# The first three stores of a streaming gradient kernel move from the SP queue to the ACT queue

## The chip, the cores and the metric

The kernel runs on one core of a Trainium2 chip. The metric is the device time of one execution in microseconds (us), as the median of several runs. Times of single steps come from one profiled execution, whose clock starts at the first instruction.

## The reference

The input `x` is a matrix of 8192 x 8192 float32 numbers, drawn at random. The result has the same shape and type.

```python
def reference(x: np.ndarray) -> np.ndarray:
    return np.gradient(x, axis=1)
```

`np.gradient` along a row means: in the inside of the row, half the difference of the right and the left neighbour; in the first column `x[1] - x[0]`, in the last column `x[m-1] - x[m-2]`. Every number of `x` is read once and every result is written once, 268.44 MB each way.

## The kernel before, in words

**Tiles.** The 8192 rows are cut into 32 tiles of 256 rows. A tile lies on 128 partitions with two whole rows on each (R = 2, m = 8192), so that one partition holds 16384 numbers, or 64 KB. One tile is 8.39 MB. A load brings a whole tile in one DMA (line 60), and a store takes a whole tile out in one DMA (line 89).

**Slots.** There are three buffers, slot0, slot1 and slot2 (NB = 3). Tile i lives in slot i mod 3. The result is written in place: a slot has 64 columns of margin in front (SH = 64), the input lies behind the margin, and the result starts at column 0. So a slot must be stored completely before the next tile can be loaded into it. `load(k)` therefore waits for the store of tile k - 3.

**The steps of one tile.** First, GpSimd (POOL) subtracts the two pairs of numbers at the row ends, for both rows, into the small tile `ends` (line 70). It waits for the load. Then VectorE (DVE) runs one custom instruction over the whole tile, half the difference of the neighbours, 128 x 16382 numbers (line 76). It also writes wrong numbers where one row meets the next, and at the row ends. Then either DVE or POOL copies `ends` over the row ends (line 87; `placer` says which of the two). Then the store is issued, which waits for that copy.

**The order of the work.** Inside `tc.manual_schedule()` each engine runs its instructions in the order in which the program text gives them. `chain` records by hand which earlier step each instruction must wait for. All 64 DMAs are issued by SyncE (SP). On SP the order is: loads 0, 1, 2, then stores 0, 1, 2, then loads 3, 4, 5, then stores 3, 4, 5, and so on, three loads and three stores in turn, up to loads 30, 31 and stores 30, 31. SP takes its instructions in order: an instruction that waits holds all that stand behind it. The loads of the next group stand behind the third store of a group because the source issues them there:

```python
if i % NB == NB - 1:
    for k in range(i + 1, min(i + 1 + NB, nsets)):
        load(k)
```

The ACT engine has no instruction of its own in this kernel, and TensorE has none either.

Of the kernel before, what the change touches and what calls it, by code (L numbers as in the profile page):

```python
# [1 line left out]

# [4 lines left out]


@with_exitstack
def kernel(  # L10
    ctx: ExitStack,
    tc: tile.TileContext,
    x: bass.AP,
    out: bass.AP,
):

    nc = tc.nc
    P = nc.NUM_PARTITIONS
    n, m = x.shape
    R = 2
    NB = 3  # L30
    SH = 64
    W = R * m
    nsets = n // (P * R)
    f32 = x.dtype

    x_sets = x.rearrange("(s p t) m -> s p (t m)", p=P, t=R)
    out_sets = out.rearrange("(s p t) m -> s p (t m)", p=P, t=R)

    pool = ctx.enter_context(tc.tile_pool(name="pool", bufs=1))
    slots = [pool.tile([P, SH + W], f32, name=f"slot{k}", tag=f"slot{k}") for k in range(NB)]  # L40
    ends = pool.tile([P, nsets, R, 2], f32, name="ends", tag="ends")
    loads, stores = [], [None] * nsets
    in_front = {}

    def chain(i, ins, *needed):

        group, engine = f"slot{i % NB}", ins.ins.engine
        keep = [o.ins for o in needed]  # L50
        if in_front.get(engine, (None,))[0] == group:
            keep.append(in_front[engine][1])
        tc.declare_no_dep(ins.ins, group=group, keep=keep, reason="implied by the needed step")
        tc.add_to_no_dep_group(group, ins.ins)
        in_front[engine] = group, ins.ins
        return ins

    def load(i):
        b = slots[i % NB]
        ins = nc.sync.dma_start(out=b[:, SH : SH + W], in_=x_sets[i])  # L60
        loads.append(chain(i, ins, *([stores[i - NB]] if i >= NB else [])))

    with tc.manual_schedule():
        for i in range(NB):
            load(i)
        for i in range(nsets):
            b = slots[i % NB]
            xin = b[:, SH : SH + W].rearrange("p (t m) -> p t m", m=m)

            ins = nc.gpsimd.tensor_sub(  # L70
                out=ends[:, i, :, :],
                in0=xin[:, :, 1 : m : m - 2],
                in1=xin[:, :, 0 : m - 1 : m - 2],
            )
            at = [chain(i, ins, loads[i])]
            ins = nc.vector._custom_dve(  # L76
                dve_ops.TENSOR_TENSOR_REDUCE_SUB_MAX,
                out=b[:, 1 : W - 1],
                in0=b[:, SH + 2 : SH + W],
                in1=b[:, SH : SH + W - 2],  # L80
                s0=0.0,
                s1=0.5,
            )
            halved = chain(i, ins, *at)
            res = b[:, 0:W].rearrange("p (t m) -> p t m", m=m)
            placer = nc.gpsimd if i % 5 in (1, 3) and i < nsets - 2 else nc.vector
            ins = placer.tensor_copy(out=res[:, :, 0 : m : m - 1], in_=ends[:, i, :, :])  # L87
            placed = chain(i, ins, halved)
            ins = nc.sync.dma_start(out=out_sets[i], in_=b[:, 0:W])
            stores[i] = chain(i, ins, placed)  # L90
            if i % NB == NB - 1:
                for k in range(i + 1, min(i + 1 + NB, nsets)):
                    load(k)


# [1 line left out]
_INS = ['x']  # L97
_OUTS = [((8192, 8192), 'float32')]


# [23 lines left out]
```

## Time and profile before

| what | value |
|---|---|
| median of 3 runs | 1247.86 us (1247.66 to 1247.92) |
| span of the profiled execution, first to last instruction | 1245.7 us |
| moved by DMA | 268.44 MB read and 268.44 MB written, mean 431 GB/s |
| DVE busy | 554.6 us, 45% of the span |
| POOL busy | 8.8 us, 1% of the span |
| one custom DVE instruction (line 76), 32 of them | 17.22 us each |
| issuing one DMA on SP | 0.34 us |

The page gives the profiled execution's own time as its span alone. The median of the runs lies 2.2 us above that span, which is what lies around the first and the last instruction. A difference that is worked out in the span is therefore added to the median.

How to read it: a line of the timeline has the start in us, the duration in us, the engine, the line of the source and the operation. "SPq" is the sequencer of SP, which only issues DMAs; a row "x3" is three issues merged, from the start of the first to the end of the third. "POOL ends L70" is the first step of a tile, and its start is within 0.1 us of the landing of the tile's load, whenever POOL was waiting for it. A DMA queue's row has the number of packets, the MB, and the time that its packets took as a share of what the 16 DMA engines have in the span.

### The profile page before, as it was taken

The page shows a single profiled execution, that of the slowest core. Times are in us where ns is not written, and L with a number is a line of the kernel's source. Part 1 is how long each engine was busy: PE and PEld are TensorE (multiplying, and loading weights), DVE is VectorE, ACT ScalarE, POOL GpSimd, SP SyncE. Part 2 cuts the span into 40 slices and gives each one's busy share as a digit, 9 for nine tenths or more (in the row PEclk, how much of TensorE's full clock was granted, in tenths as well). Part 3 has the DMA queues.
Part 4 walks back from the last instruction along what each step waited for, and adds up shares of the span by engine and source line. Part 5 has one row for each costly group of instructions (what it writes and reads, how often), then busy time and mean ns, then how long its engine had stood idle before and what let it go on. Part 6 is the DMA issues. An engine that isn't in the chain of part 4 may idle for free.

```text
span 1245.7 us, 237 instructions
## 1 busy us (share of the span) xinstructions
DVE 554.6 (45%) x52; POOL 8.8 (1%) x48
## 2 busy tenths in 40 slices
DVE  2850583069009702850582079009603840591083
POOL 0000000000000000000000000000000000000000
DMA  9999999999999999999999999999999999999999
GB/s 404 438 436 423 427 431 438 438 438 436 436 427 431 425 438 436 425 434 436 429 434 436 434 436 434 436 434 438 419 436 436 434 438 438 431 434 429 429 410 404
DMA packets 9217, 536.88 MB, mean 431 GB/s; under 512 B 1024, under 2 KB 1024, under 8 KB 1024
## 3 DMA queue, kind: packets, MB, share of 16 engines
q1 hardware_dynamic: 9216, 536.88, 99.8%
q14 instruction: 1, 0.01, 0.0%
HBM read 268.44 MB, written 268.44 MB: 431 GB/s over the span
## 4 chain that ended last, share of the span: by engine, by line
another core or an unknown queue 74%; DVE 18%; DMA 3%; issue 2%; POOL 1%; SPq 0%; POOLq 0%
DVE slot L76 18%; DMA slot<-in_x_dram 3%; POOL ends L70 0%; POOL slot L87 0%; SPq L60 0%; POOLq L119 0%; DVE slot L87 0%
## 5 line engine op out<-in xcount | busy, mean ns | idle before, releaser
L76 DVE CUSTOM_DVE_ANT_0 slot<-slot 128x16382 f32<-128x16382 f32 x32 | 551.2, 17224 | 668.7 <-POOL ends L70 668.7
L70 POOL TENSOR_TENSOR ends<-slot 128x4 f32<-128x4 f32 x32 | 6.3, 198 | 989.6 <-DMA slot<-in_x_dram 989.6
L87 POOL COPY slot<-ends 128x4 f32<-128x4 f32 x12 | 2.3, 190 | 207.9 <-DVE slot L76 207.9
L87 DVE COPY slot<-ends 128x4 f32<-128x4 f32 x20 | 3.4, 172 | 0.7
L108 POOL MEMSET const-bfloat16-1.0<- 128x1 bf16 x1 | 0.1, 101 | 0.0
L108 POOL MEMSET const-uint8-127<- 128x1 uint8 x1 | 0.1, 101 | 0.0
L108 POOL MEMSET const-float32-0.0<- 128x1 f32 x1 | 0.1, 98 | 0.2 <-issue 0.2
L108 POOL MEMSET const-float32-1.0<- 128x1 f32 x1 | 0.1, 98 | 0.0
## 6 DMA issues: line engine op xcount, KB each, us to landing
slot<-in_x_dram SPq DMA_DIRECT2D x32, 58.0
out_dram<-slot SPq DMA_DIRECT2D x32, 40.4
```

Of the source, the lines that this page charges most:

```text
L70: ins = nc.gpsimd.tensor_sub(out=ends[:, i, :, :], in0=xin[:, :, 1 : m : m - 2], in1=xin[:, :, 0 : m - 1 : m - 2],)
L76: ins = nc.vector._custom_dve(dve_ops.TENSOR_TENSOR_REDUCE_SUB_MAX, out=b[:, 1 : W - 1], in0=b[:, SH + 2 : SH + W], in1=b[:, SH : SH + W - 2],
L87: ins = placer.tensor_copy(out=res[:, :, 0 : m : m - 1], in_=ends[:, i, :, :])
L108: nc = _bacc.Bacc("TRN2", target_bir_lowering=False, num_devices=1)
```

## The change

The stores of tiles 0, 1 and 2 are issued by the ACT engine instead of SP. All other stores stay on SP. The waits are the same as before: store i still waits for the row ends to be placed, and load i + 3 still waits for store i. Because the three stores are gone from SP, loads 3, 4 and 5 now stand directly behind loads 0, 1 and 2 there, each with its wait for its store. Behind load 5 come stores 3, 4, 5, and from there on the order is that of before. On ACT there are the three stores and nothing else.

```diff
             placed = chain(i, ins, halved)
-            ins = nc.sync.dma_start(out=out_sets[i], in_=b[:, 0:W])
+            queue = nc.scalar if i < NB else nc.sync
+            ins = queue.dma_start(out=out_sets[i], in_=b[:, 0:W])
             stores[i] = chain(i, ins, placed)
```

Empty lines were taken out as well, so that the line numbers of the changed kernel are smaller: its loads are on line 49, its stores on line 79, the custom DVE instruction on line 65, the first POOL step on line 59.

## The prediction

> **What bounds the kernel now.** I read the engines and the DMA queues on the page first, then the queue's waits, then the timeline of SP and POOL, then windows of the opening.
>
> ```profile
> DVE 554.6 (45%) x52; POOL 8.8 (1%) x48
> DMA packets 9217, 536.88 MB, mean 431 GB/s; under 512 B 1024, under 2 KB 1024, under 8 KB 1024
> q1 hardware_dynamic: 9216, 536.88, 99.8%
> ```
>
> One queue, q1, carries all 64 transfers, and its packets fill 99.8% of the 16 DMA engines' time. No compute engine is above 45%. Of the 9216 packets 1024 are tiny, which leaves 8192 of 536.88 MB / 8192 = 65.5 KB: a partition's 64 KB is one packet, and a transfer is 128 of them, eight on each DMA engine (with one tiny one behind).
>
> ```profile
> SPq L60 <- DMA out_dram<-slot: 373.1, 29, 19.3
> 0.74 1.33 SPq L60 DMA_DIRECT2D slot<-in_x_dram  x3
> 40.40 40.06 SPq L89 DMA_DIRECT2D out_dram<-slot  x3
> 81.78 39.38 SPq L60 DMA_DIRECT2D slot<-in_x_dram  x3
> 157.63 39.09 SPq L89 DMA_DIRECT2D out_dram<-slot  x3
> 197.97 39.21 SPq L60 DMA_DIRECT2D slot<-in_x_dram  x3
> ```
>
> The first row says that SP waited 373.1 us in 29 loads for a store. These waits cost nothing, because the ring holds transfers meanwhile: load 3 is issued at 81.78, when stores 1 and 2 (issued at 59.8 and 80.1) still lie ahead of it, 2 x 19.3 us of work. The same holds in each group. The kernel is bound by DMA time alone: what counts is how long a packet takes, and whether an engine ever finds both rings empty.
>
> ```profile
> 42.04 0.20 POOL L70 TENSOR_TENSOR ends<-slot 128x4 f32<-128x4 f32 x1 [19.13 <-DMA slot<-in_x_dram]
> 62.44 0.20 POOL L70 TENSOR_TENSOR ends<-slot 128x4 f32<-128x4 f32 x1 [2.69 <-DMA slot<-in_x_dram]
> 391.81 0.20 POOL L70 TENSOR_TENSOR ends<-slot 128x4 f32<-128x4 f32 x1 [19.16 <-DMA slot<-in_x_dram]
> 411.86 0.20 POOL L70 TENSOR_TENSOR ends<-slot 128x4 f32<-128x4 f32 x1 [19.85 <-DMA slot<-in_x_dram]
> ```
>
> The starts of line 70 are landings of loads. Load 1 lands 42.04 - 22.71 = 19.33 us after load 0: eight packets of 2.42 us, which I take as the undisturbed price. But load 2, the last load ahead of a store, takes 62.44 - 42.04 = 20.40, which is 1.07 more, and load 11, again the last ahead of a store, 411.86 - 391.81 = 20.05. I worked out the same for the last load of each of the ten full groups: 1.07, 0.13, 0.19, 0.73, 0.53, 0.47, 0.13, 0.52, 0.01 and 0.04 us over 19.32. The trace's records of single packets put this extra on the eighth packet of that load, on nearly every engine (up to 3.82 us against 2.42), and no packet behind it makes it up: none is under 2.415. I call it the price of a turn from load to store. The turn from store to load costs less: in the same records the first packets of a group's first load have 0.02 us more on average.
>
> ```profile
> 1.00:42.00 41.00, 17.39 (x2) 0.20 (x1) 1.00 1.02 435
> 42.00:62.00 20.00, 17.23 (x1) 0.39 (x2) 1.00 1.02 416
> 62.00:120.00 58.00, 17.40 (x2) 0.20 (x1) 1.00 1.00 434
> ```
>
> The windows (last column GB/s) show the same from the other side: 435 while only loads run, 434 while only stores run, 416 in the 20 us that hold the first turn, while the DMA share stays full. So the engines are "busy" in a turn, and slower.
>
> **The change part by part.** *Bytes and transfers.* The same 64 transfers run; 64 x 19.32 = 1236.5 us of packets cannot be saved by a queue's name. *Issues.* Three issues of 0.34 us leave SP and stand on ACT, which has nothing else to do. Either way they lie beside running transfers: 0. Only their waits for line 87 are queued on ACT, with nothing behind them but the next store. *Loads 3, 4, 5.* They stand earlier on SP but not earlier in time: each still waits for the store that empties its slot. What stands behind load 5 now is store 3: it is ready once load 3 has landed and DVE has run 17.2 us on it, before load 5 can be issued at about 160, and load 5 itself covers 19.3 us of DMA time. So it comes in time: 0. From there the order is the old one.
>
> The Trainium skill ("DMA: Bandwidth & Descriptors", section "Issuing engines are not separate DMA queues") says that DMAs from several engines interleave on the same 16 engines and that issuing from a second one saves only sequencer time; by that rule the change can gain at most nothing here, and no row of this trace, with its one queue, shows such an interleaving.
>
> *What the opening becomes.* Before, the 16 engines ran load 2, then stores 0, 1, 2, then loads 3, 4, 5, in blocks. Now store 0 comes to a second ring at 40.4, when load 2 is about to begin on the first. If the two rings are served by turns, both run from 42 at half rate and end at about 42 + 2 x 19.3 = 81. Store 1 (issued at about 59.6) follows on its ring; load 3 is issued at 81 and comes 1.6 us later (the last store, alone, is issued at 1223.97 and takes 20.9 us to land: 20.9 - 19.3). Load 2 landed at 81 means store 2 is issued at 81 + 17.2 + 0.6 = 99, long before store 1 ends at about 119. Load 3 beside store 1 and load 4 beside store 2 go on in the same manner to about 158, then load 5 is issued, and the old blocks follow. In that stage, 42 to 158, six transfers of 19.3 us take their 116 us as before, if a packet costs the same.
>
> *Turns.* With rings that alternate packet by packet, each of the 3 x 8 = 24 load packets of an engine has a store packet behind it: 24 turns in place of the one at 62 us (the turn from load 5 to store 3 is in both). The trace has no two rings at work, so the price of such a turn is bounded by the ten turns above: 0.01 to 1.07 us. The first and dearest came while all engines were in step; of the nine later ones the median is 0.19, and I take that, since alternating packets will bring the engines out of step at once. 24 x 0.19 = 4.6, less the 1.07 of the turn that goes: +3.5 us. At the lower end it is 24 x 0.01 - 1.07 = -0.8, at the upper 24 x 1.07 - 1.07 = +24.6, and at 0.47, the upper middle of the ten, +10.2.
>
> *A gap ahead of load 5.* Load 5 is issued when store 2 has ended. If load 4 has ended by then, both rings are empty for 1.6 us, plus some 0.6 for engines that ended early. With even service load 4 began 1.6 us later than store 2 and so covers this: I take 0, and 0 to 2.2 for the range.
>
> Sum against the profiled execution: 1245.7 + 3.5 = 1249.2 us of span; the median of the runs lies 2.2 above the span, so 1247.86 + 3.5 = **1251.4**.
>
> In the skill, the same page's section "Queues, rings and completion order" says that an engine drains a whole packet, typically 9 to 17 descriptors, from one ring before it goes to the next. If that packet is a whole transfer's share (nine records per engine here), the stage would run load 2, stores 0 and 1, load 3, store 2, loads 4 and 5: one turn more than before, an estimated +0.2 us instead of +3.5. The profile's count of packets, one for 64 KB, speaks for the finer alternation, and nothing here settles it.
>
> **The rivals.** *Turns between two rings cost nothing, or come once per transfer.* For it: turns at 993 and 1109 us cost 0.01 and 0.04. Against it: eight of ten cost 0.13 or more. It gives -1.07 to +0.2, so 1246.8 to 1248.1: no change, and so not slower.
>
> *Two rings hide each other's latency.* Packets of one direction could fill what the other leaves, so that the stage's 48 packets per engine run quicker. To be faster by 2.5 us the stage's 116 us would have to lose 1.4 us besides the turn of 1.07, 1.2% of a packet. With 2% it is -1.07 - 2.3 = -3.4: 1244.5. Against it: no packet under 2.415 us in 8192, and no slice of the page above 438 GB/s.
>
> *Every turn is as dear as the first, or one ring outruns the other and leaves gaps.* All engines in step through the stage give 24 x 1.07 = 25.7 less 1.07: 1272.5. Gaps alone give 2.2 at most ahead of loads 3, 4 and 5 each: 6.6 - 1.07 = +5.5, 1253.4.
>
> *The change does not do what it says* can be left out: in the built program ACT holds the three stores, and SP six loads in a row.
>
> **How the numbers follow.** A measurement of this kernel can tell about 0.2%, 2.5 us, from no change. The forecast (alternating packets, turns of 0.15 to 0.6 us, +2.5 to +13) has 0.48. Free or few turns: 0.33, all within 0.2%. Hidden latency: 0.07, faster. Dear turns or gaps: 0.12, slower. So faster 0.07, same 0.33, slower 0.60. The range starts at 1246.6, just under the free turns, which leaves out the faster case, and ends at 1262, 24 turns of 0.63 us; it leaves out the dearest turns. The forecast's own range is 1250.4 to 1261.
>
> **What would show it.** The changed profile should have two rows of hardware queues, one of 432 packets and 25.2 MB. Tile 2 should land at about 82 instead of 62.4, load 3 at about 121 instead of 139.9, and load 5 should be issued near 160 instead of 120.8. Tile 6, which landed at 256.2, should land 3 to 4 us later, and all later landings by the same: the whole cost lies ahead of 160 us. Windows from 45 to 155 should be at about 420 GB/s, against 434. If tile 2 lands at 62 still, rings are served by whole transfers. If tile 6 lands at 255 to 256.5, turns are free; if the DMA share dips near 159, it is the gap. A kernel that loses its time after 250 us, or is slower with the opening unchanged, would prove the whole reading wrong.

## The result and the profile after

The changed kernel takes 1250.84 us (median of 21 runs, 1249.29 to 1252.36). The kernel before, run beside it, takes 1248.03 us (21 runs). The ratio is 1.0022, with a 95% interval of 1.0016 to 1.0028: slower by 2.8 us. A profiled execution of the changed kernel has a span of 1248.4 us and a time of 1250.30, so 1.9 us lie around the span; the 2.2 given for the kernel before sets the median of three runs against the span of one. The ratios below, but not the medians, leave out two single executions that were far slower than the others of their kernel (1283.9 us in the first experiment, 1268.6 in the sixth).

The head of the page and its DMA queues, after:

```profile
span 1248.4 us, 237 instructions
q1 hardware_dynamic: 8784, 511.71, 94.9%
q10 hardware_dynamic: 432, 25.17, 4.7%
```

There are two queues now. 432 packets are three transfers of 144, the three stores on ACT. The sum of the shares is 99.6% against 99.8%.

The timeline of SP (a row is start, duration, what; x2 and x3 are merged):

```profile
117.84 39.12 SPq L49 DMA_DIRECT2D slot<-in_x_dram  x2
157.06 43.31 SPq L79 DMA_DIRECT2D out_dram<-slot  x3
201.64 0.34 SPq L49 DMA_DIRECT2D slot<-in_x_dram  x1
```

Load 4 is issued at 117.84 and load 5 at 117.84 + 39.12 - 0.33 = 156.63, where it had been 120.83. Store 3 follows at once, at 157.06. Load 6 comes at 201.64; it had been 197.97, so the opening has already cost 3.7 us here.

The landings of the tiles, as starts of the first POOL step (line 59 now):

```profile
42.12 0.20 POOL L59 TENSOR_TENSOR ends<-slot 128x4 f32<-128x4 f32 x1 [19.15 <-DMA slot<-in_x_dram]
79.20 0.20 POOL L59 TENSOR_TENSOR ends<-slot 128x4 f32<-128x4 f32 x1 [19.38 <-DMA slot<-in_x_dram]
122.77 0.20 POOL L59 TENSOR_TENSOR ends<-slot 128x4 f32<-128x4 f32 x1 [43.36 <-DMA slot<-in_x_dram]
159.09 0.20 POOL L59 TENSOR_TENSOR ends<-slot 128x4 f32<-128x4 f32 x1 [18.61 <-DMA slot<-in_x_dram]
182.35 0.20 POOL L59 TENSOR_TENSOR ends<-slot 128x4 f32<-128x4 f32 x1 [23.07 <-DMA slot<-in_x_dram]
259.63 0.20 POOL L59 TENSOR_TENSOR ends<-slot 128x4 f32<-128x4 f32 x1 [77.08 <-DMA slot<-in_x_dram]
```

Tiles 4, 5 and 6 in the kernel before:

```profile
159.25 0.20 POOL L70 TENSOR_TENSOR ends<-slot 128x4 f32<-128x4 f32 x1 [1.65 <-DMA slot<-in_x_dram]
178.70 0.20 POOL L70 TENSOR_TENSOR ends<-slot 128x4 f32<-128x4 f32 x1 [19.25 <-DMA slot<-in_x_dram]
256.24 0.20 POOL L70 TENSOR_TENSOR ends<-slot 128x4 f32<-128x4 f32 x1 [77.34 <-DMA slot<-in_x_dram]
```

Tile 2 lands at 79.20 instead of 62.44, since load 2 shares the engines with store 0. The comparison that counts is load 5: when it has landed, both kernels have moved the same nine transfers (loads 0 to 5 and stores 0 to 2). It lands at 182.35 against 178.70, 3.65 us later. Load 4, just ahead of it, is not late at all: 159.09 against 159.25, with the same eight transfers done in both kernels. The time is lost in the 23.3 us between these two landings, which had been 19.45. Tile 6 lands 259.63 - 256.24 = 3.39 us later, and the last tile 1208.96 - 1206.28 = 2.68 us later.

The windows of the opening (the last column is GB/s), first of the kernel before, then of the changed one:

```profile
120.00:185.00 65.00, 40.69 (x4) 0.79 (x4) 1.00 0.99 426
```

```profile
62.00:120.00 58.00, 17.40 (x2) 0.20 (x1) 1.00 1.00 434
120.00:185.00 65.00, 37.03 (x4) 0.79 (x4) 1.00 0.99 417
```

From 62 to 120 us, with loads and stores alternating all the time, the rate is 434 GB/s, as it was with stores alone. From 120 to 185 it is 417 against 426.

The records of single packets say where. From 47 us to about 116 every engine takes a 64 KB packet from one queue, then from the other (but for four store packets in a row around 80 us, before load 3 has begun), in 2.418 us each: the alternating turns cost nothing. There are 20 of them per engine, counting each store packet that follows a load packet up to load 5. Three places are dear. The packet of load 2 ahead of the first store packet takes 3.0 to 3.7 us; that is the first turn, as before. The last packet of load 5, ahead of store 3, takes 3.3 to 4.3 us on all 16 engines, about 1.4 more than 2.418; before, that place cost 0.2. And around 158 us the first packets of load 5 take up to 0.7 us more, and one engine stands idle for 2.0 us ahead of them; on 12 of the 16 the last packet of load 4 just lasts until load 5 begins. On the mean engine load 5 is done 1.6 us later than before (179.88 against 178.24 in the landing records); the rest of the 3.65 us is the one engine.

### The profile page after: what moved, and what is told of

The parts are those of the page before. It is cut to its first block, busy times and chain, and to the rows that moved or that the text cites. A ratio compares the mean times of both kernels' runs of the same rounds, so it can differ in the third digit from the quotient of the medians.

```text
span 1248.4 us, 237 instructions
## 1 busy us (share of the span) xinstructions
DVE 554.6 (44%) x52; POOL 8.8 (1%) x48
## 4 chain that ended last, share of the span: by engine, by line
another core or an unknown queue 72%; DVE 17%; DMA 7%; issue 2%; POOL 1%; SPq 0%; POOLq 0%
DVE slot L65 17%; DMA slot<-in_x_dram 4%; DMA out_dram<-slot 3%; POOL ends L59 0%; POOL slot L76 0%; SPq L49 0%; DVE slot L76 0%; POOLq L109 0%
```

## The experiments

Three theories stood at the outset. A: the ring that runs dry ahead of load 5 costs, by itself and by the dear turn behind it; alternation is free. B, the step of the forecast: each of the alternating turns costs. C: two rings put the engines in step, and that makes the next block's turn dear.

**1. All stores on ACT.**

```diff
-            queue = nc.scalar if i < NB else nc.sync
+            queue = nc.scalar
```

> All 32 stores on ACT, so that two rings alternate to the end and no store stands behind a load. Theory A (dry rings): alternating turns are free after the first; what the change costs is the moment ahead of load 5 when both rings run dry, and the dear turn at the end of a block of loads that began on dry rings. Here no ring runs dry and there are no blocks, so only the first turn's 1.07 us stays of the 3.82 us that the ten turns of before cost: 1248.0 - 2.75 = 1245.3 us, 1244.3 to 1246.5, faster than both kernels. Theory B (the forecast's step: each of the alternating turns costs; +2.8 + 1.07 us over 24 turns is 0.16 us each): 29 x 8 = 232 turns more, 37 us less 3.8: about 1281 us. Theory C (two rings put the engines in step, and a block's turn after that is dear): as A, since there is no block.

Measured: 1252.92 us, 1.0056 of the kernel before (1.0024 to 1.0088). B falls: it asked for 1281. But A is wrong by 7.6 us as well. The timeline shows the greater part at the end:

```profile
1211.51 0.20 POOL L59 TENSOR_TENSOR ends<-slot 128x4 f32<-128x4 f32 x1 [38.43 <-DMA slot<-in_x_dram]
1211.74 17.22 DVE L65 CUSTOM_DVE_ANT_0 slot<-slot 128x16382 f32<-128x16382 f32 x1 [21.20 <-POOL ends L59]
1229.21 0.34 ACTq L79 DMA_DIRECT2D out_dram<-slot  x1
```

Load 31 lands at 1211.51, DVE needs 17.22 us, and store 31 is issued at 1229.21. Meanwhile only the rest of store 30 is left, which had run beside load 31: by the packet records 13 of the 16 engines end it between 1220.3 and 1221.0 and stand idle for 9.1 to 9.9 us. Up to there alternation is cheap: between 185 and 1190 us a mean engine loses 0.9 us in all by packets that take more than 2.418 us, where the kernel before loses 2.1.

A second thing was not in any theory. The records of the landings, which have a time for each of the 16 engines, show the engines drifting apart: the share of store 0 lands within 0.62 us on all engines, that of store 6 within 5.94, that of store 16 within 11.15. The landings of loads, on the other queue, stay within 4 us. So an engine may serve more of one ring and less of the other than its neighbours, and a store is complete, and the next load of its slot can go, only when the last engine has done its share.

**2. The first 15 stores on ACT.**

```diff
-            queue = nc.scalar if i < NB else nc.sync
+            queue = nc.scalar if i < 5 * NB else nc.sync
```

> The first 15 stores on ACT in place of 3, one hand-over back to the single ring (load 17). Theory A: one dry moment and one dear turn as in the changed kernel, wherever the hand-over stands, and the four cheap block turns at loads 5, 8, 11 and 14 of before (0.13 + 0.19 + 0.73 + 0.53 = 1.6 us) are gone: 1250.8 - 1.6 = 1249.2 us, 1248.2 to 1250.3; load 17 lands about 23 us after load 16, and the turn behind it shows in its last packets. Theory B: five times as many alternating turns, 120 x 0.16 = 19 us less 1.07 and 1.6: about 1264 us. Theory C: as A.

Measured: 1253.7 us, 1.0049 (1.0037 to 1.0061). B's 1264 falls again, with five times as many alternating turns. A's 1249.2 is 4.5 us too low. At the hand-over to one ring, load 17 waits for store 14:

```profile
590.21 0.20 POOL L59 TENSOR_TENSOR ends<-slot 128x4 f32<-128x4 f32 x1 [38.42 <-DMA slot<-in_x_dram]
626.36 0.20 POOL L59 TENSOR_TENSOR ends<-slot 128x4 f32<-128x4 f32 x1 [35.95 <-DMA slot<-in_x_dram]
647.08 0.20 POOL L59 TENSOR_TENSOR ends<-slot 128x4 f32<-128x4 f32 x1 [3.02 <-DMA slot<-in_x_dram]
```

The 16 shares of store 14 land between 617.05 and 623.80 us. Fifteen engines idle for 1.1 to 4.2 us ahead of load 17, and load 17's last packet is dear again (3.3 to 3.9 us): it lands 20.72 us after load 16, though 15 engines began it before load 16's last share had landed. The dry moment is longer than in the changed kernel, and the engines had come further apart by then. Two later turns of this profile (loads 26 and 29) together cost 1.7 us more than those of before, which I can't put down to the edit.

**3. The hand-over in halves.** Store 2 and load 5 are two DMAs each, and the first half of load 5 waits for the first half of store 2 only.

```diff
+            ins = nc.sync.dma_start(out=b[:, SH : SH + cut], in_=x_sets[i][:, 0:cut])
+            first = chain(i, ins, half[0])
+            ins = nc.sync.dma_start(out=b[:, SH + cut : SH + W], in_=x_sets[i][:, cut:W])
+            loads.append((first, chain(i, ins, half[0], stores[i - NB])))
```

> The changed kernel, with store 2 and load 5 cut into two DMAs each, so that the first half of load 5 waits for the first half of store 2 only and is in the ring before the rings run dry. Everything else as in the changed kernel. Theory A: no dry moment, and the turn from load 5 to store 3 costs what a block turn of before does, 0.0 to 0.7 us in place of about 1.5 at the slowest engine: 1248.0 us, 1247.4 to 1249.0; tile 6 lands within 0.8 us of 256.3. Theory B: the 24 alternating turns stay, so it stays at 1250.8, 1250.0 to 1251.6, tile 6 at 259.6. Theory C: the dry moment goes (0.4 us on the mean engine, 2.2 at most), the dear turn stays: 1249.5 to 1250.5.

Measured: 1250.57 us, 1.0027 (1.0017 to 1.0036). A's 1248.0 is missed, and the profile, of the slowest run of this kernel (1253.04), says why: the edit moved the dry moment and did not remove it.

```profile
148.94 0.33 SPq L52 DMA_DIRECT2D slot<-in_x_dram  x1
169.72 0.33 SPq L54 DMA_DIRECT2D slot<-in_x_dram  x1
```

The second half of load 5 (line 54) is issued at 169.72. On 15 engines the second half of store 2 had landed by 164.56; on the 16th it landed at 169.70, because that one engine had come out of step. The others were through with everything at 167.4 to 167.8 and idled for 2.9 to 4.1 us. So this run decides nothing on the dear turn, but it shows the price of one engine out of step.

**4. Three dry moments on a single ring.** The kernel before; from tiles 9, 15 and 21 on the slots are renamed so that the load needs the slot of the tile just ahead of it.

```diff
+    def slot_of(i):
+        return (i + 2 * sum(i >= d for d in (9, 15, 21))) % NB
...
-        b = slots[i % NB]
+        b = slots[slot_of(i)]
```

> The kernel before, all on SP, with the slots renamed from tiles 9, 15 and 21 on so that loads 9, 15 and 21 need the slot of the tile just ahead of them and wait for stores 8, 14 and 20, the last ones in the ring: the one ring runs dry three times, with no second ring anywhere. Theory A: each dry moment costs 1.6 to 2.2 us by itself and makes the turn at the end of that block dear, 1.0 to 1.9 us in place of 0.73, 0.47 and 0.52: 3 x 3.3 - 1.7 = +8, so 1256 us, 1254 to 1258.6; loads 11, 17 and 23 land 20.3 to 21.2 us after loads 10, 16 and 22. Theory C: a dry ring costs only itself, 3 x 1.6 to 2.2: 1252.8 to 1254.6, with loads 11, 17 and 23 at 19.4 to 20.0. Theory B says the same as C.

Measured: 1257.93 us, 1.0084 (1.0071 to 1.0097), or +10.5. A asked for +8 (1254 to 1258.6), B and C for 1254.6 at most. The landings around the first of the three:

```profile
376.33 0.20 POOL L76 TENSOR_TENSOR ends<-slot 128x4 f32<-128x4 f32 x1 [62.12 <-DMA slot<-in_x_dram]
395.68 0.20 POOL L76 TENSOR_TENSOR ends<-slot 128x4 f32<-128x4 f32 x1 [19.15 <-DMA slot<-in_x_dram]
416.14 0.20 POOL L76 TENSOR_TENSOR ends<-slot 128x4 f32<-128x4 f32 x1 [20.26 <-DMA slot<-in_x_dram]
```

Load 9 lands 79.83 us after load 8, where 77.28 is undisturbed: 2.55 for the dry moment (2.79 and 2.60 in the other two). Load 11 lands 416.14 - 395.68 = 20.46 after load 10, 1.13 over 19.33 (loads 17 and 23: 1.53 and 1.24). The sum is 7.94 + 3.90 = 11.84, less the 1.72 that these three turns cost in the kernel before: +10.1 of the +10.5. One dry moment costs 2.6 us by itself and 1.3 at the end of the block, without any second ring. The ten full groups' other turns in this profile: the kernel's first, which also follows a dry start, 1.46; the six others 0.02 to 1.04. These are the prices at the slowest engine. The mean over the 16 engines, from the packet records, parts the two kinds clearly: 1.1 to 1.4 us at the end of a block that began on a dry ring (load 2 before and here, loads 11, 17 and 23 here, load 17 in experiment 2, load 5 in three profiles of the changed kernel), at most 0.7 at every other block turn of these profiles.

**5. Store 3 ahead of load 5.** The changed kernel, with this order on SP.

```diff
-            if i % NB == NB - 1:
+            for k in {NB - 1: (3, 4), 3: (5,), 4: (6,), 5: (7, 8)}.get(i, ()):
+                load(k)
+            if i > 5 and i % NB == NB - 1:
```

> The changed kernel with the opening's order on SP changed: loads 3, 4, store 3, load 5, store 4, load 6, store 5, loads 7, 8, and from store 6 on as before. Stores 0, 1, 2 stay on ACT with their 24 alternating turns. Store 3 is ready at about 141, so that it lies in SP's ring behind load 4 when store 2 ends, and 19 us of work cover load 5's late issue and any engine that is out of step. Theory A (the ring that runs dry ahead of load 5 is what costs, by itself and through the turn behind it): the cost goes, but for two more turns on a running ring at 0.0 to 0.7 us each: 1248.0 us, 1247.2 to 1249.2; no load's last packets take over 3.2 us before 300 us but those ahead of store 0. Theory B (alternating turns cost) and theory C (having used two rings makes the next turn dear): it stays at 1250 to 1251.6.

Measured: 1249.26 us, 1.0014 (1.0005 to 1.0023), between the 1247.2 to 1249.2 of A and the 1250 to 1251.6 of B and C, and nearer to A. The profile is of the fastest run (1247.09, span 1245.2, half a microsecond under the kernel before):

```profile
158.83 0.20 POOL L59 TENSOR_TENSOR ends<-slot 128x4 f32<-128x4 f32 x1 [18.48 <-DMA slot<-in_x_dram]
197.70 0.20 POOL L59 TENSOR_TENSOR ends<-slot 128x4 f32<-128x4 f32 x1 [38.67 <-DMA slot<-in_x_dram]
```

Load 5 now lands 38.87 us after load 4, with store 3 in between: 38.64 is the undisturbed price of the two. Both the dry moment and the dear turn at 175 us are gone, with the same 20 alternating turns on two rings. B and C can't explain this run. The edit also leaves a single load ahead of each of the next turns, so it is experiment 4, with blocks of three throughout, that ties the dear turn to the dry ring. What its slower runs lose is the question of experiments 10 and 11.

**6. All stores on ACT but the last two.**

```diff
-            queue = nc.scalar if i < NB else nc.sync
+            queue = nc.scalar if i < nsets - 2 else nc.sync
```

> All stores on ACT as in the first experiment, but stores 30 and 31 on SP behind load 31. In the first experiment the rings stood dry for 9.6 us ahead of store 31 (store 30 had run beside load 31 and was done before tile 31 was). Here store 30 runs alone behind load 31 and covers tile 31's compute. Theory A (alternation is free, dry rings cost): 1252.9 - 9 = 1244 to 1246 us, faster than before. Theory B (alternating costs by itself, 5 us over the whole kernel as the first experiment's time could also be read): 1251 to 1253.

Measured: 1247.91 us, 1.0021 (0.9996 to 1.0046): not to be told from the kernel before. The median misses A's 1244 to 1246 and B's 1251 to 1253. Five of its eleven runs are under 1247.6, the best at 1244.99 is as A forecast and under every run of the kernel before, but others reach 1256.9 and 1261.6. The only profile is of the execution of 1268.6: its loads land up to 20 us apart over the 16 engines and its stores up to 22.5, against 3.9 and 12.5 in experiment 1. That is one execution, left out of the ratio; that the runs between 1250 and 1261.6 lose their time in the same way is not shown. This version has the lower floor and no hold on it, and beats nothing.

**7. One ring, one load and one store in turn.** An edit of the kernel before.

```diff
-            if i % NB == NB - 1:
-                for k in range(i + 1, min(i + 1 + NB, nsets)):
-                    load(k)
+            if i >= 1 and i + 2 < nsets:
+                load(i + 2)
```

> The kernel before with another order on SP, and no second ring: loads 0, 1, 2, stores 0, 1, then load 3, store 2, load 4, store 3 and so on, one load and one store in turn; no ring runs dry, since each issue has another transfer ahead of it. 30 turns from load to store in place of 11. If a turn on a running ring has the price of the nine later ones of before (mean 0.31 us): 19 x 0.31 = +5.9, 1253.4 us, 1250 to 1256. If a turn is paid once behind a dry start and is then free as long as directions change often (what the alternating packets of two rings show): the nine turns of before go, -2.75: 1244.7 us, 1243.7 to 1246.5.

Measured: 1250.4 us, 1.0024 (1.0015 to 1.0034): at the low end of the first range, 3.0 under its 1253.4, and clear of the second. Tile 31 lands at 1208.35, 2.07 us later than before, behind the same 62 transfers: 29 turns cost 3.82 + 2.07 = 5.9 us, and without the first (0.97) the other 28 cost 0.18 us each, with the changes from store to load in the sum. On one ring a turn is neither free nor as dear as the mean of before.

**8 and 9. The changed kernel again,** without an edit.

> The changed kernel once more, for a second profile. If the dry ring ahead of load 5 is the cause, load 5 lands 22.5 us or more after load 4 again, though it has the rings for itself at the end, and tile 6 lands 2.5 to 4 us later than 256.2. If the first profile showed a chance event, tile 6 lands within 1 us of 256.2.

> The changed kernel, for a third profile. The same as for the second: load 5 lands 22.5 us or more after load 4 and tile 6 lands 2.5 to 4 us later than 256.2 if the dry ring is the cause, within 1 us of it if not.

Both profiles have 1248.3 us of span. Load 5 lands 181.48 - 158.67 = 22.81 us after load 4 in the third, as expected; in the second 181.32 - 160.54 = 20.78, because load 4 itself was late by 1.3 us with one engine out of step by 1.6 us. The third:

```profile
158.67 0.20 POOL L59 TENSOR_TENSOR ends<-slot 128x4 f32<-128x4 f32 x1 [18.50 <-DMA slot<-in_x_dram]
181.48 0.20 POOL L59 TENSOR_TENSOR ends<-slot 128x4 f32<-128x4 f32 x1 [22.61 <-DMA slot<-in_x_dram]
```

Against the kernel before load 5 is late by 2.62 and 2.78 us, tile 6 by 2.36 and 2.49 (a little less than the 2.5 I had set), and the last tile by 2.61 and 2.63. In all three profiles the last packet of load 5 takes 3.2 to 4.3 us on nearly every engine. The loss is no chance event; how it is shared between the dry moment and an engine out of step changes from run to run.

**10 and 11. Store 3 ahead of load 5 again,** the kernel of experiment 5.

> Store 3 ahead of load 5 once more, for a second profile: its runs reached from 1247.1 to 1252.3, and the first profile was of the fastest one. If one DMA engine that gets out of step with the other 15 in the stage of two rings costs the rest, a slower run here shows landings of stores 1 and 2 whose last engine comes over 1.5 us after the 15th, and loses its time there; if the profile is of a fast run, the spread stays at 0.6 us as in the first.

> Store 3 ahead of load 5, for a third profile. The same as for the second: a slower run shows an engine whose share of stores 1 and 2 lands over 1.5 us after the 15th, a fast run shows a spread of 0.6 us over all 16.

Spans of 1247.4 and 1247.1 us; on the same chip the changed kernel had 1248.3 twice and the kernel before, run once, 1244.9. Apart from one packet of 3.0 to 3.1 us on the engine that is out of step, in neither is there a dry moment or a dear turn between 156 and 185 us. But load 5 is late by 2.2 us or more against the first profile (200.01 and 199.93, where it was 197.70). In experiment 11 one engine's share of stores 1 and 2 lands 3.6 and 3.8 us after the 15th engine's, as expected. In experiment 10 the engine that is out of step comes 0.7 us after the 15th in store 2 and 1.4 us in load 4, which is less than the 1.5 I had asked for; the place agrees, the size only in part. An engine that is behind stays behind: the shares of store 5 still land 3.2 us apart in both, the last at 258.1. By then both orders have moved the same thirteen transfers as the kernel before when its load 6 has landed. The mean engine has lost nothing there: its share lands at 255.57 and 255.56, against 255.59 before. So up to that point the loss of these two profiles comes from engines that are out of step alone.

## Why the prediction was right, and where not

The time was forecast at 1251.4 and came at 1250.84, and the loss is there when load 6 lands. But it does not lie where the prediction had it, spread over the stage of two rings and wholly ahead of 160 us: in the first profile load 4 was 0.16 us early at 159 us, and all of the loss came between 159 and 182. The windows from 45 to 155 us, forecast at 420 GB/s against 434, read 429 in both kernels. The sum reached its number by the wrong terms.

*What held.* DMA time alone sets the end. Nothing is saved by a second queue, and the issues cost nothing. The stage of two rings went by turns, packet by packet: store 0 beside load 2, load 3 beside store 1, load 4 beside store 2, with tile 2 at 79.2 (forecast 82) and load 5 issued at 156.6 (forecast near 160). From load 6 on the old order came back, and the later landings kept 2.2 to 3.4 us.

*What failed: the turns.* The step "24 x 0.19 = 4.6, less the 1.07 of the turn that goes" is wrong in its count and in both terms. There were 20 such turns, since some load packets have a load packet behind them. The 19 behind the first cost nothing that the packet records show (2.418 us each), and experiments 1 and 2, with ten and five times as many, rule out 0.16 us each. And the 1.07 does not go: the first turn is still there, at 44 us in place of 58. I took the price of a turn from turns between blocks of three transfers. Experiment 7 gives 0.18 for turns between single transfers on one ring; for packets of two rings it is zero.

*What failed: the gap.* "I take 0" for the gap ahead of load 5 is the term that was mis-sized. It was worked out as if all engines ran alike: load 4 was to cover 1.6 us. On 12 engines it did, but one idled for 2.0 us and three for 0.2 to 0.3, and the price did not end there. "The turn from load 5 to store 3 is in both" put nothing down for that turn; on the mean engine it cost 0.2 before and 1.4 after. A block of loads that begins on dry rings ends with a dear turn; experiment 4 shows this on one ring alone, 2.6 us for the dry moment and 1.3 for the turn. In the changed kernel these two and an engine out of step make up the 2.6 to 3.65 us by which load 5 is late in three profiles. Experiment 5, which takes away the dry ring and keeps the alternation, takes 1.1 of the 2.8 us away in the median (+1.7 stays), and all of it in the run whose engines stayed together. The rest goes with single engines that come out of step while two rings run, as in experiments 10 and 11; no part of the prediction had them. How the parts share the 2.8 us of the median is not settled: in two profiles of the changed kernel the engines were still within 0.6 us at load 4 and parted only at the dry moment. That the sum of the two wrong terms came out at +3.5 is luck.

*The rivals.* The rival of free turns was right about the turns and wrong about the time. The rival of gaps had the right place, priced at 2.2 per gap; it named the cause most closely and was given 0.12 together with the dear turns. No packet of the changed kernel was quicker than 2.418 us, which disposes of hidden latency.

The Trainium skill ("DMA: Bandwidth & Descriptors", section "Queues, rings and completion order") says that an engine drains a whole packet of typically 9 to 17 descriptors from one ring before it switches. Here the engines switched after each record of 64 KB, so for these rows the trace decides against a transfer's whole share as the unit. The same page (section "Why a DMA increments its semaphore by 16 and not by 1") says that the 16 engines of a DMA finish independently and only the full count means that all data has landed; this agrees with the spreads seen here, where load 5 waited for the last of 16 shares of store 2 (in experiment 3, of its second half, 5.1 us behind the other 15).

*Open.* Why a block of loads that began on a dry ring ends with a turn of 1.1 to 1.4 us on the mean engine was not shown, only that it does so in the profiles counted in experiment 4. The engine need not have idled: in the changed kernel 12 engines went from load 4 to load 5 without a gap of 0.15 us, with nothing queued between, and paid the dear turn all the same. What throws single engines out of step on two rings isn't shown either.

## What to carry to other kernels

Where DMA time is the bound, look for the moment when a ring runs dry, and price it with what follows: in experiment 4, 2.6 us for the wait and 1.3 for the next change of direction. A hand-over from two queues to one is such a moment when the next transfer on the remaining queue waits for the last one on the other; put a transfer that is already free ahead of it (here that won back 1.1 of the 2.8 us). And price a two-queue stage by its slowest engine, since a transfer is complete only when all 16 shares have landed.

## What the hardware showed that was not expected

Loads and stores that alternate packet by packet on two queues run at 434 GB/s with no price for the change of direction, while changes between whole transfers on one queue cost 0.18 us (experiment 7) to 0.38 (the ten of the kernel before) on average. With two queues the 16 engines drift apart: shares of one store landed within 0.6 us at first and within 12.5 us at the end of experiment 1 (in the kernel before, 0.6 us at first and never more than 3.05), and executions of experiments 1 and 6 spread from 1245.0 to 1266.3 us, without the two that the ratios leave out, where the kernel on one queue stays within 1246.9 to 1249.7.
